# A hybrid encoder step on one core: values product with two heads in the column halves, and three smaller moves

## Chip, cores and metric

The kernel runs on one core of one Trainium2 chip. The metric is device time in microseconds (us), the median of the runs shown; lower is better.

## What is computed

One inference step of a one-layer streaming encoder on 2048 prompt frames and on 8 sampled streams of 16 frames, all float32, model width 1024. Three residual sub-layers follow one another: a mixer, a cross-attention into 256 memory tokens, and a squared-ReLU MLP. The change is in the mixer alone. Cut to it:

```python
q, k, v, u = in_proj(rms_norm(xp, g_mix_pre), w_in)      # 8 heads of 64; u = a * sigmoid(b), 512 channels
s = einsum('bnqhd,bnkhd->bnhqk', qc, kb) * Dh ** -0.5    # each 64-frame chunk against a 576-frame key band
s = where(key_valid, s + rel_bias(table, q_off, k_off), NEG_INF)
o = einsum('bnhqk,bnkhd->bnqhd', softmax(s), vb)
c = depthwise_conv(pad(u, 30), w_dw) + b_dw              # width 31, causal
c = silu(group_layer_norm(c, ln_g, ln_b))
xp = xp + rms_norm(concat([rms_norm(o), rms_norm(c)]) @ w_out, g_mix_post)
```

A sampled stream attends to 128 cached frames and its own 16, and its convolution continues from 30 cached rows.

## The kernel before, in words

**Layout of the work.** The 16 prompt tiles of 128 frames and the one tile of sampled frames form four query blocks, QT: tiles 0 to 3 and the sampled tile, then 4 to 7, 8 to 11 and 12 to 15. For each block the input projection (`glu`, `qk`, `vv`) multiplies the transposed rows by column pieces of w_in. Each product is made in three passes of high and low halves (`mm3`, line 122; `split`, lines 94 and 95, makes the halves: ACT the high, DVE or POOL the low). Queries, keys and values go to the DRAM scratch tensors Qd, Kd and Vd.

**Order.** A planner (`Plan`) holds closures with due times; `add(t0, t1, fns)` spreads a list of them evenly over an interval, `run` calls them in order of time, and the constants PAR give the intervals. So the input projection of block q + 1, the attention of block q, and the convolution taps are interleaved on PE, DVE, ACT and POOL, each of which takes its work in order. Loads and most stores are issued on SP's queue, also in order. A framework places the tiles into a fixed number of buffers per tag and adds the waits; a tile whose buffers are all in use waits for one to come free, and so does what stands behind it on the same queue.

**Attention (`attn`, lines 533 to 623).** For block q and head h, `attn_load` (line 533) loads the queries (tag aq), the keys in two transfers (ak), the values (av) and the bias table (ab); every one of these tags has two buffers. The planner's list goes through the 8 heads, each with its 4 query tiles, one step per tile. `scores` (551) makes up to 640 scores for 128 queries in the one score tile in PSUM (tag sc, one buffer of two banks); DVE adds the bias and takes the minimum (570), ACT exponentiates (573). One step later `xpose` (579) transposes the probabilities 128 x 128 at a time into one of three transpose banks (tag tp), and ACT copies them out into a tile of tag apt (two buffers). Two steps later `values` (592) multiplies with the probabilities as weights and the head's values as the moving operand:

```python
    for j in range(nj):
        nc.tensor.matmul(oc[:, i, :], pt[:, j, :], vt[:, jo + j, :], start=j == 0, stop=j == nj - 1)
```

Here pt[:, j, :] is 128 x 128 and vt[:, jo + j, :] is 128 x 64; a float32 matmul appears in the profile as two records. After a head's fourth tile DVE takes reciprocals of the sums (604) and scales the result (606), and after every second head SP stores 128 columns into the scratch catd (609). `attn` adds the load of head h + 1 behind step 2 of head h.

**Convolution.** `glu` (316) writes u of block q behind 30 carried columns in a tile of 542. For q above 0, POOL copies them from the carry tile ucar (326), and at the end of the block POOL copies the last 30 columns into ucar (340). The 31 taps of each of four channel groups run on DVE (452), block by block. Eight u tiles exist.

**Sampled streams (`sattn`, lines 629 to 719).** Before block 0's attention, eight streams are taken in turn. `sattn_load` (654) loads a stream's cached keys (tag att, shared with the biased scores) and values (tag sv), POOL places the queries into a zero-padded tile (664), PE transposes the keys (667) and ACT copies them out (668). The products with four heads side by side (677 and 703) use column tiles 32 wide, set by `tile_position`.

**After the mixer's attention** come the output projection (`out_norm`, `out_t`, `out_b`), which begins during block 3's attention, the memory attention and the MLP.

## Time and profile before

| what | value |
|---|---|
| median of 3 runs | 3248.61 us (3243.86 to 3252.39) |
| profiled execution, its own time | 3248.02 us |
| its span, first to last instruction | 3246.2 us |
| PE (matmul) busy | 3116.6 us, 96% |
| PEld (weight load) busy | 2659.1 us, 82% |
| DVE busy | 1820.0 us, 56% |
| ACT busy | 1234.3 us, 38% |
| POOL busy | 604.6 us, 19% |
| mean granted TensorE clock | 0.984 of full |

PE is TensorE's matmul, PEld its weight load, which overlaps PE; DVE is VectorE, ACT ScalarE, POOL GpSimd, SP SyncE, and a trailing q (SPq) means the engine's instruction queue. Matmuls are pipelined and their ends are modelled, so a PE that is shown busy need not be PE at its peak. The shares are means over stages that differ; a table by stage says more. L599 is line 599 of the kernel before.

### The profile page before, as it was taken

The numbers are of one execution on the slowest core, as the hardware profiler recorded it, in microseconds if no ns is written. First come the engines' busy times: TensorE is split into PE (matmuls) and PEld (weight loads), VectorE is DVE, ScalarE is ACT, GpSimd is POOL, SyncE is SP. The second block draws the span as 40 slices with busy tenths as digits, with TensorE's granted clock in tenths as the row PEclk, the third lists the DMA queues.
The fourth block names the chain that finished last, engine by engine and source line by source line (L and its number), as shares of the span: only waits on it lengthen the run. The fifth ranks groups of instructions, "written<-read, shape, count | busy, mean of one in ns | idle before, by whom it ended". The sixth has DMA issues, their size and how long they took to land. (4 is left out here: it accounts for less than half of the span.)

```text
span 3246.2 us, 44496 instructions
## 1 busy us (share of the span) xinstructions
PE 3116.6 (96%) x16628; PEld 2659.1 (82%) x16628; DVE 1820.0 (56%) x2807; ACT 1234.3 (38%) x2498; POOL 604.6 (19%) x655
## 2 busy tenths in 40 slices
PE   7987989999899999999999999999999999999998
PEld 7875878979798768788888999988888888888887
DVE  6797989788534435433335444456445544465444
ACT  3233454544554435322234232334334333343332
POOL 4346253442222320122211000002000200020000
PEclk9998999999899999999999999999999999999999
DMA  5464666747865565222224222234233433243222
GB/s 190 127 181 136 185 180 166 194 126 188 248 166 170 187 210 174 88 72 65 62 91 140 82 75 82 75 110 153 88 104 120 143 104 101 88 141 122 91 95 75
DMA packets 295062, 421.49 MB, mean 130 GB/s; under 512 B 54968, under 2 KB 163520, under 8 KB 294774
## 3 DMA queue, kind: packets, MB, share of 16 engines
q1 hardware_dynamic: 286286, 387.71, 40.4%
q0 software_dynamic: 8560, 30.94, 2.4%
q8 instruction: 131, 2.15, 0.3%
q14 instruction: 85, 0.70, 0.1%
HBM read 352.93 MB, written 69.52 MB: 130 GB/s over the span
## 5 line engine op out<-in xcount | busy, mean ns | idle before, releaser
L122 PE MATMUL pu<-xT,wu 128*128 128x512 f32 (+1 forms) x3840 | 756.6, 358 | 0.3 <-ACT wu L94 0.3
L122 PE MATMUL pd<-wd,h 128*128 128x512 f32 x3264 | 750.1, 390 | 0.1
L122 PEld LDWEIGHTS pu<-xT,wu 128*128 128x128 f32 x3840 | 660.2, 188 | 92.8 <-ACT wu L94 0.8
L122 PEld LDWEIGHTS pd<-wd,h 128*128 128x128 f32 x3264 | 611.4, 188 | 127.9 <-DVE y L1348 0.5
L122 PE MATMUL pm<-xT,w 128*128 128x512 f32 (+3 forms) x1992 | 427.1, 366 | 12.7 <-POOL w L95 4.2
L452 DVE SCALAR_TENSOR_TENSOR acc<-u,wdT,acc 128x512 f32<-128x512 f32 x480 | 429.4, 895 | 6.2
L103 POOL TENSOR_SCALAR nm<-nss 128x1 f32<-128x1 f32 x103 | 30.8, 299 | 2009.6 <-ACT nsq L132 1069.8
L122 PEld LDWEIGHTS pm<-xT,w 128*128 128x128 f32 x1992 | 341.5, 196 | 58.7 <-POOL w L95 5.2
L94 ACT ACTIVATE wd<-wst 128x512 fp32r<-128x512 f32 x256 | 159.9, 632 | 429.7 <-PE pd L122 365.3
L95 POOL TENSOR_TENSOR w<-wst,w 128x512 fp32r<-128x512 f32 x154 | 235.6, 1546 | 350.6 <-ACT w L94 320.5
L1348 DVE TENSOR_TENSOR y<-pd,y 128x512 f32<-128x512 f32 x238 | 163.8, 688 | 207.1 <-PE pd L122 207.1
L1330 DVE SCALAR_TENSOR_TENSOR hh<-pu,r 128x512 f32<-128x512 f32 (+1 forms) x160 | 96.9, 609 | 325.1 <-ACT r L1329 324.9
L1329 ACT ACTIVATE r<-pu 128x512 f32<-128x512 f32 (+1 forms) x160 | 84.0, 529 | 370.5 <-PE pu L122 364.8
L95 DVE TENSOR_TENSOR wu<-wst,wu 128x512 fp32r<-128x512 f32 x256 | 170.8, 690 | 83.9 <-ACT wu L94 82.6
L122 PE MATMUL pm<-wo,cT 128*128 128x512 f32 x816 | 200.2, 397 | 0.0
L95 DVE TENSOR_TENSOR wd<-wst,wd 128x512 fp32r<-128x512 f32 x256 | 178.9, 723 | 32.9 <-ACT wd L94 32.1
L94 ACT ACTIVATE wu<-wst 128x512 fp32r<-128x512 f32 x256 | 157.5, 631 | 96.3 <-DMA wst<-w_ffn_up 62.6
L122 PE MATMUL y<-mo,pT 128*128 128x512 f32 x768 | 186.8, 397 | 0.0
L122 PE MATMUL sc<-m,xT 128*128 128x512 f32 x768 | 182.0, 392 | 0.3 <-ACT xT L94 0.2
L122 PEld LDWEIGHTS pm<-wo,cT 128*128 128x128 f32 x816 | 151.1, 188 | 33.6 <-issue 2.9
L122 PEld LDWEIGHTS y<-mo,pT 128*128 128x128 f32 x768 | 142.8, 188 | 33.1
L122 PEld LDWEIGHTS sc<-m,xT 128*128 128x128 f32 x768 | 142.9, 188 | 30.7 <-DVE xT L95 0.5
(248 smaller groups left out, 3597.1 us busy)
## 6 DMA issues: line engine op xcount, KB each, us to landing
wst<-w_ffn_up SPq DMA_DIRECT2D x256, 256.0 KB, 3.2
wst<-w_ffn_down SPq DMA_DIRECT2D x256, 256.0 KB, 3.0
wst<-w_in SPq DMA_DIRECT2D x160, 256.0 KB, 3.3
ak<-Kd SPq DMA_DIRECT2D x48, 512.0 KB, 6.7
ab<-biasd SPq DMA_DIRECT2D x32, 320.0 KB, 4.2
cx<-catd SPq DMA_DIRECT2D x17, 512.0 KB, 5.3
x1d<-oy POOLq DMA_DIRECT2D x17, 512.0 KB, 6.4
nx<-x1d SPq DMA_DIRECT2D x17, 512.0 KB, 3.6
```

What stands on the lines that cost most here:

```text
L94: nc.scalar.activation(hi, src, AF.Copy)
L95: return (lo_eng or nc.vector).tensor_sub(lo, src, fr(hi))
L103: nc.gpsimd.tensor_scalar(m, ss, 1.0 / count, EPS, op0=ALU.mult, op1=ALU.add)
L122: self.nc.tensor.matmul(out, lhs(a), rhs(b), start=first and n == 0, stop=last and n == 2)
L452: i = nc.vector.scalar_tensor_tensor(o, s, wdT[:, c, w:w + 1], o, op0=ALU.mult, op1=ALU.add)
L1329: nc.scalar.activation(r, pm, AF.Relu)
L1330: nc.vector.scalar_tensor_tensor(hh, pm, 0.0, r, op0=ALU.max, op1=ALU.mult)
L1348: nc.vector.tensor_add(y, pm, y)
```

## The change

Five parts go together.

1. The values product swaps its operands: the head's values are the weights (64 columns) and the transposed probabilities move (128 columns). Two heads of a pair g are multiplied alternately, one into the lower 64 partitions of oc and one into the upper 64, with `tile_position=(0, x * HD)`. The result is transposed, heads' dimensions by queries, and fills a whole PSUM bank. After the fourth query tile ACT copies it out, and a new closure `heads_out` transposes it back tile by tile on PE into a transpose bank, from which DVE scales it for both heads at once; SP stores it.
2. The steps of the two heads of a pair are interleaved in the order ORDER. `values` of a query tile follows two steps behind the second head's scores, `heads_out` three steps behind the last. Heads 0 and 1 of a block are loaded first; head h + 2 is loaded behind the last score step of head h. Tags av and apt have four buffers in place of two.
3. The carry tile ucar goes. The first 30 columns of a block's u are copied, at the start of the block, from the tile of the block before.
4. A sampled stream's cached keys are loaded one stream ahead (`sattn_keys`, from tag av), its values go to tag ab, and the query tile to tag aq.
5. ACT, not POOL, places the sampled queries.

```diff
--- before.py
+++ after.py
...
@@ -258,7 +258,6 @@
-            ucar = [vp.tile([P, 30], F32, tag=f"ucar{c}", name=f"ucar{c}", bufs=1) for c in range(4)]
@@ -323,7 +322,7 @@
                             else:
-                                nc.gpsimd.tensor_copy(U[q, c][:, 0:30], ucar[c])
+                                nc.gpsimd.tensor_copy(U[q, c][:, 0:30], U[q - 1, c][:, 512:542])
                         nc.scalar.activation(U[q, c][:, 30 + c0:30 + c0 + npr], pm[:, :npr], AF.Copy, scale=0.5)
@@ -336,8 +335,6 @@
-                        if c0 + n >= 512 and q < 3:
-                            nc.gpsimd.tensor_copy(ucar[c], u[:, 512:542])
@@ -540,12 +537,13 @@
                         nc.sync.dma_start(fr(kt)[j * HD:(j + 1) * HD, :, :nk * P], Kd[h, :, :, k0 * P:(k0 + nk) * P].rearrange("a d t -> d a t"))
-                    vt = mp.tile([P, 8, HD], F32, tag="av", name="av")
+                    vt = mp.tile([P, 8, HD], F32, tag="av", name="av", bufs=4)
                     nc.sync.dma_start(vt[:, :nk, :], Vd[k0 * P:(k0 + nk) * P, h].rearrange("(j p) d -> p j d", p=P))
                     nc.sync.dma_start(bt, biasd[h])
-                    ss = mp.tile([P, 4], F32, tag="ass", name="ass")
-                    KQ[q, h] = (qt, kt, vt, bt, ss, k0)
+                    if h % 2 == 0:
+                        SUM[q, h // 2] = mp.tile([P, 4, 2], F32, tag="ass", name="ass")
+                    KQ[q, h] = (qt, kt, vt, bt, SUM[q, h // 2], k0)
                 return fn
@@ -570,7 +568,7 @@
-                    nc.scalar.activation(pr[:, :n], tt[:, :n], AF.Exp, bias=mn, scale=-1.0, accum_out=ss[:, i:i + 1])
+                    nc.scalar.activation(pr[:, :n], tt[:, :n], AF.Exp, bias=mn, scale=-1.0, accum_out=ss[:, i, h % 2:h % 2 + 1])
@@ -579,7 +577,7 @@
                 nj = n // P
-                pt = mp.tile([P, 5, P], F32, tag="apt", name="apt")
+                pt = mp.tile([P, 5, P], F32, tag="apt", name="apt", bufs=4)
                 for a, b in ((0, min(nj, 3)), (3, nj)):
@@ -587,39 +585,64 @@
                             nc.tensor.transpose(tp[:, (j - a) * P:(j - a + 1) * P], pr[:, j * P:(j + 1) * P], self.ident)
                         dst, src = pt[:, a:b, :], tp.rearrange("p (j q) -> p j q", j=b - a)
                         nc.scalar.activation(dst, src, AF.Copy)
-                READY.append((q, h, i, pt, nj, jo))
-            def values():
-                q, h, i, pt, nj, jo = READY.pop(0)
-                qt, kt, vt, bt, ss, k0 = KQ[q, h]
-                if i == 0:
-                    OC[q, h] = ps.tile([P, 4, HD], F32, tag="oc", name="oc")
-                oc = OC[q, h]
-                for j in range(nj):
-                    nc.tensor.matmul(oc[:, i, :], pt[:, j, :], vt[:, jo + j, :], start=j == 0, stop=j == nj - 1)
-                if i == 3:
-                    if h % 2 == 0:
-                        A[q] = mp.tile([P, 4, P], F32, tag="a", name="a")
-                    r = mp.tile([P, 4], F32, tag="ar", name="ar")
+                READY[q, h, i] = pt, nj, jo
+            def values(q, g, i):
+                def fn():
+                    if i == 0:
+                        OC[q, g] = ps.tile([P, 4, P], F32, tag="oc", name="oc")
+                    oc = OC[q, g]
+                    hs = [READY.pop((q, 2 * g + x, i)) + (KQ[q, 2 * g + x][2],) for x in range(2)]
+                    nj = hs[0][1]
+                    for j in range(nj):
+                        for x, (pt, _, jo, vt) in enumerate(hs):
+                            nc.tensor.matmul(oc[x * HD:(x + 1) * HD, i, :], vt[:, jo + j, :], pt[:, j, :], start=j == 0, stop=j == nj - 1,
+                                             tile_position=(0, x * HD))
+                    if i == 3:
+                        ot = mp.tile([P, 4, P], F32, tag="t512", name="ot")
+                        nc.scalar.activation(ot, oc, AF.Copy)
+                        OC[q, g] = ot
+                return fn
+            def heads_out(q, g):
+                def fn():
+                    ot, ss = OC.pop((q, g)), SUM.pop((q, g))
+                    tp = ps.tile([P, 512], F32, tag="tp", name="tpv", bufs=TPB)
+                    for i in range(4):
+                        nc.tensor.transpose(tp[:, i * P:(i + 1) * P], ot[:, i, :], self.ident)
+                    r = mp.tile([P, 4, 2], F32, tag="ar", name="ar")
                     nc.vector.reciprocal(r, ss)
-                    c = (h % 2) * HD
-                    nc.vector.tensor_tensor(A[q][:, :, c:c + HD], oc, r.unsqueeze(2).to_broadcast([P, 4, HD]), op=ALU.mult)
-                    if h % 2:
-                        t0 = QT[q][0]
-                        nc.sync.dma_start(catd[t0 * P:(t0 + 4) * P, (h - 1) * HD:(h + 1) * HD].rearrange("(i p) c -> p i c", p=P), A[q])
+                    A = mp.tile([P, 4, P], F32, tag="a", name="a")
+                    nc.vector.tensor_tensor(A.rearrange("p i (x d) -> p (i x) d", x=2), tp.rearrange("p (n d) -> p n d", d=HD),
+                                            r.rearrange("p i x -> p (i x)").unsqueeze(2).to_broadcast([P, 8, HD]), op=ALU.mult)
+                    t0 = QT[q][0]
+                    nc.sync.dma_start(catd[t0 * P:(t0 + 4) * P, g * P:(g + 1) * P].rearrange("(i p) c -> p i c", p=P), A)
+                return fn
+            ORDER = ((0, 0), (0, 1), (1, 0), (0, 2), (1, 1), (0, 3), (1, 2), (1, 3))

             def attn(q):
-                fns = [attn_load(q, 0)]
-                for n in range(4 * H + 2):
-                    h, i = n // 4, n % 4
-                    if n < 4 * H:
-                        fns.append(scores(q, h, i))
-                    if 0 < n <= 4 * H:
+                steps = [(2 * g + x, i) for g in range(H // 2) for x, i in ORDER]
+                fns = [attn_load(q, 0), attn_load(q, 1)]
+                for n in range(len(steps) + 3):
+                    if n < len(steps):
+                        fns.append(scores(q, *steps[n]))
+                    if 0 < n <= len(steps):
                         fns.append(xpose)
-                    if n > 1:
-                        fns.append(values)
-                    if i == 2 and h + 1 < H:
-                        fns.append(attn_load(q, h + 1))
+                    if 1 < n < len(steps) + 2:
+                        h, i = steps[n - 2]
+                        if h % 2:
+                            fns.append(values(q, h // 2, i))
+                    if n > 2:
+                        h, i = steps[n - 3]
+                        if h % 2 and i == 3:
+                            fns.append(heads_out(q, h // 2))
+                    if n < len(steps):
+                        h, i = steps[n]
+                        if i == 3 and h + 2 < H:
+                            fns.append(attn_load(q, h + 2))
                 return fns


@@ -641,7 +664,7 @@
-                SA["q"] = q = mp.tile([P, 4, P], F32, tag="saT", name="saq", bufs=1)
+                SA["q"] = q = mp.tile([P, 4, P], F32, tag="aq", name="saq")
@@ -650,18 +673,24 @@
                 z = mp.tile([P, 2, 4, 32], F32, tag="sqb", name="sz", bufs=1)
                 nc.gpsimd.memset(z, 0.0)
                 SA["z"] = [z[:, n] for n in range(2)]
+                sattn_keys(0)
+            def sattn_keys(b):
+                SA["ck", b] = ck = mp.tile([P, DA], F32, tag="av", name="sck", bufs=4)
+                nc.sync.dma_start(ck, I["cache_attn_k"][0, b].rearrange("t h d -> t (h d)"))

             def sattn_load(b):
                 def fn():
-                    ck = mp.tile([P, DA], F32, tag="att", name="sck")
-                    nc.sync.dma_start(ck, I["cache_attn_k"][0, b].rearrange("t h d -> t (h d)"))
-                    cv = mp.tile([P, DA], F32, tag="sv", name="scv")
+                    ck = SA.pop(("ck", b))
+                    if b + 1 < 8:
+                        sattn_keys(b + 1)
+                    cv = mp.tile([P, 640], F32, tag="ab", name="scv")[:, :DA]
                     nc.sync.dma_start(cv, I["cache_attn_v"][0, b].rearrange("t h d -> t (h d)"))
                     K, Z = SA["k"][b % 2], SA["z"][b % 2]

                     for j in range(2):
                         rs = slice(j * HD, (j + 1) * HD)
-                        nc.gpsimd.tensor_copy(Z[rs, :, j * 16:(j + 1) * 16], SA["q"][rs, :, b * 16:(b + 1) * 16])
+                        nc.scalar.activation(Z[rs, :, j * 16:(j + 1) * 16], SA["q"][rs, :, b * 16:(b + 1) * 16], AF.Copy)
                     pt = ps.tile([P, 512], F32, tag="tp", name="pt", bufs=TPB)
                     for p in range(4):
                         nc.tensor.transpose(pt[:, p * P:(p + 1) * P], ck[:, p * P:(p + 1) * P], self.ident)
@@ -695,7 +724,7 @@
-                    PT = mp.tile([P, 2, P], F32, tag="apt", name="spt")
+                    PT = mp.tile([P, 2, P], F32, tag="apt", name="spt", bufs=4)
...
```

Two hunks that give the setup tiles of tag av four buffers as well, and one that renames dictionaries, are left out.

## Rows read from the trace of the kernel before

**Rows 1.** Stages: us from the start, length; busy (records) per engine; clock; DMA share; GB/s.

```profile
205.00:315.00 110.00, 86.45 (x546) 65.00 (x545) 91.31 (x151) 42.83 (x91) 64.76 (x68) 0.94 0.56 161
315.00:430.00 115.00, 107.00 (x726) 94.77 (x725) 108.44 (x196) 56.66 (x152) 34.54 (x24) 0.99 0.69 185
430.00:680.00 250.00, 232.26 (x1448) 206.32 (x1447) 204.51 (x285) 116.91 (x253) 114.12 (x92) 0.97 0.63 167
680.00:850.00 170.00, 159.24 (x1083) 145.77 (x1083) 138.29 (x218) 82.23 (x184) 44.74 (x36) 0.97 0.68 183
850.00:1000.00 150.00, 143.20 (x905) 129.54 (x906) 65.60 (x123) 85.15 (x202) 33.85 (x46) 0.94 0.65 177
```

The engines of these rows are, in this order, PE, PEld, DVE, ACT and POOL.

**Rows 2.** The same stages, instructions of line 599 alone: PE, PEld, clock, DMA.

```profile
315.00:430.00 115.00, 21.28 (x152) 20.24 (x152) 0.99 0.69 185
430.00:680.00 250.00, 41.60 (x328) 40.74 (x328) 0.97 0.63 167
680.00:850.00 170.00, 39.36 (x320) 39.19 (x320) 0.97 0.68 183
850.00:1000.00 150.00, 42.20 (x320) 41.42 (x320) 0.94 0.65 177
```

**Rows 3.** Timeline of PE, merged: start us, length us, line, tiles, count.

```profile
564.85 1.23 PE L599 MATMUL oc<-av,apt 128*128 128x64 f32 x10
565.89 0.83 PE L566 MATMUL sc<-ak,aq 128*128 128x320 f32 x4
566.56 0.71 PE L587 MATMUL tpa<-ident,apr 128*128 128x128 f32 x5
...
845.78 0.49 PE L587 MATMUL tpa<-ident,apr 128*128 128x128 f32 x3
846.11 2.34 PE L599 MATMUL oc<-av,apt 128*128 128x64 f32 x20
```

**Rows 4.** Waits of DVE, 430 to 680: us in total, times, longest us.

```profile
DVE lnd L506 <- POOL lnr L105: 9.7, 7, 2.1
```

**Rows 5.** Timeline of PE around a sampled stream's values product.

```profile
259.11 0.43 PE L703 MATMUL ov<-scv,spt 128*32 128x128 f32 x8
259.35 0.40 PE L703 MATMUL ov<-svn,spt 128*32 128x128 f32 x8
259.69 0.49 PE L486 MATMUL pt<-cent,acc 128*128 128x128 f32 x2
```

**Rows 6.** Line 703: duration in ns, min/median/max, first and last start.

```profile
L703 PE MATMUL ov<-svn,spt x64: 272/273/423, 238.3 to 316.5; 128*32 128x128 f32 x64
```

**Rows 7.** Timeline of DVE in block 3's attention, two score steps three apart.

```profile
922.08 0.82 DVE L570 CUSTOM_DVE_ANT_0 att<-sc,ab 128x640 f32<-128x640 f32 x1 [0.22 <-PE sc L566]
...
929.58 0.82 DVE L570 CUSTOM_DVE_ANT_0 att<-sc,ab 128x640 f32<-128x640 f32 x1 [0.32 <-ACT apr L573]
```

**Rows 8.** Groups by line, 0 to 1300: busy us, mean ns; idle before, releaser.

```profile
L606 DVE TENSOR_TENSOR a<-oc,ar 128x256 f32<-128x256 f32 x32 | 13.4, 419 | 15.1 <-PE oc L599 15.0
L570 DVE CUSTOM_DVE_ANT_0 att<-sc,ab 128x512 f32<-128x512 f32 x8 | 5.5, 682 | 0.0
L488 ACT ACTIVATE lnd<-pt 128x512 f32<-128x512 f32 x17 | 10.0, 592 | 25.4 <-PE pt L486 13.4 <-DMA catd<-lnd 6.8 <-PE pt L667 5.2
L340 POOL COPY ucar<-u 128x30 f32<-128x30 f32 x12 | 5.4, 454 | 25.5 <-DVE u L335 25.5
```

**Rows 9.** Waits of SP's queue, 850 to 1000.

```profile
SPq L544 <- PE oc L599: 45.6, 4, 14.9
```

**Rows 10.** Timeline of SP's queue: one head's load.

```profile
878.64 0.36 SPq L539 DMA_DIRECT2D aq<-Qd  x1
879.04 1.25 SPq L542 DMA_DIRECT2D ak<-Kd  x2
```

**Rows 11.** DMA issues by line: count, KB each, median us to landing.

```profile
ak<-Kd SPq DMA_DIRECT2D x48, 512.0 KB, 6.7
```

**Rows 12.** Waits of PE, 205 to 315.

```profile
PE pt L667 <- DMA sck<-cache_attn_k: 10.1, 5, 3.1
```

More of the change, by code (lines that the diff above doesn't have):

```diff
@@ L231, in bias_tables @@
                 for h in range(H):
-                    hk = mp.tile([P, 2, P], F32, tag="av", name="hk")
+                    hk = mp.tile([P, 2, P], F32, tag="av", name="hk", bufs=4)
                     for m in range(2):
@@ L243, in bias_tables @@
                     nc.sync.dma_start(biasd[h], bt)
-                hs = mp.tile([P, 2, P], F32, tag="av", name="hs")
+                hs = mp.tile([P, 2, P], F32, tag="av", name="hs", bufs=4)
                 nc.sync.dma_start(hs[:, 0, :].rearrange("p (h q) -> p h q", h=H), view(extd, P, [[1, P], [768, H], [1, 16]]))
@@ L528, in lns @@
                 return fns
-            A, KQ, PEND, READY = {}, {}, [], []
+            KQ, SUM, PEND, READY = {}, {}, [], {}
             def attn_load(q, h):
```

## Prediction, made before the change was run

> **What bounds the kernel now.** I first cut the span into the stages in which the changed code runs [rows 1]: the sampled streams' attention (205 to 315 us), the band attention of query blocks 0, 1 and 2, each interleaved with the input projection of a later block (315 to 430, 430 to 680, 680 to 850), and that of block 3, interleaved with the output projection (850 to 1000). The reader is to see which engine is nearly full. From 315 to 850 both PE and DVE are: DVE is busy 108.4 of 115, 204.5 of 250 and 138.3 of 170 us, because the convolution taps run there. From 850 to 1000 there are no taps; DVE is busy 65.6 of 150 us, PE 143.2. Everything after 1000 us is outside the change; I take it to move as a block.
>
> Next I asked how much of these stages is the values product of line 599 [rows 2]: 152, 328, 320 and 320 matmul records, 1120 in all. The merged timeline [rows 3] gives their pace: ten take 1.23 us, twenty 2.34, so one per 0.111 us and 124.3 us of PE for all. Three transposes take 0.49 us, five 0.71: 0.11 each.
>
> The waits say what DVE does in its idle time. In 430 to 680 its largest wait is for POOL, 9.7 of 45.5 idle us [rows 4], a round trip that a faster PE does not shorten. So PE time saved in the last stage should show, before it only partly.
>
> **Values as weights.** Removed are the 1120 records with 128 weight columns and 64 moving ones. Added are as many with 64 weight columns and 128 moving, two heads side by side in the column halves: 560 rounds of two. The trace has no tile 64 columns wide, but four tiles 32 wide with 128 moving columns [rows 5]: 16 records in four rounds, the first at 259.11, the last ending at 259.75 and lasting 0.27 [rows 6], so starting at 259.48. Three rounds in 0.37 us make 0.12 a round, loading of weights included. The bounds are 0.111 (the pace of one matmul) and 0.222 (two in turn); I take 0.12, the row nearest in shape. 560 x 0.12 = 67.2, which saves 57.1 us.
>
> The Trainium skill, TensorE: Matmul & The Clock Gate, Part 3, lists as seen that weights are loaded beside matmuls in flight only where the row group differs, which column halves do not. By that a round would be a load and then its matmuls, the 0.222 of the rival on halves in turn, and the sum 3260; by the row it is 0.12, and the sum is the one below. Four rounds with all their loads at 0.12 do not agree with the rule.
>
> Entering and leaving the column tiles costs something too. The next whole-array matmul starts at 259.69 [rows 5], 0.21 after the last round began, where a round takes 0.12: 0.09 lost. I take as much on the way in, rounded to 0.2 for both. Four blocks, four pairs of heads and four query tiles make 64 visits: 12.8 us, or twice that if other work is put between the parts of a visit. The result now comes out transposed, so each of the 16 pairs needs four transposes back: 64 x 0.11 = 7.0 us. Net on PE: 57.1 - 12.8 - 7.0 = 37.3 us less, 0.0333 per record, with ends of 54 less (rounds of 0.111, free switches) and 20 more (rounds of 0.222).
>
> How much reaches the end depends on the stage. By [rows 2] the shares are 5.1, 10.9, 10.7 and 10.7 us.
> In 850 to 1000 PE is the bound, but there is one score buffer: scores take 0.83 us [rows 3], the reduction that frees their buffer 0.82 [rows 7], so steps that follow closely cannot come faster than 1.65 us and two hand-overs, against 2.26 us of PE work today (values 1.04, scores 0.67, transposes 0.55, by the starts and paces of [rows 3]). Two thirds: 7.1. In 680 to 850 and 430 to 680 DVE idles 19% and 18%, partly for reasons that stay; half: 5.4 and 5.5. In 315 to 430 DVE idles only 6.6 us; a fifth: 1.0. Sum: 19.0 us.
>
> **Scaling moves to the pair.** DVE had 32 scalings of 0.419 us [rows 8], 13.4 us. Now there are 16 of 512 columns out of PSUM, which I price by the 128x512 reduction of 0.682: 10.9. 2.5 us less, half of it in stages where DVE is full: 1.3. Sixteen reciprocals of a few elements go too; left out. ACT gains 16 copies of 0.592 us [rows 8], 9.5 us, which its idle time hides (busy 341 of 685 us from 315 to 1000, rows 1). What they hold is scarcer: a 512-column buffer shared with the gates and the normalisation, and one of three transpose banks until DVE has scaled. Between 0 and 3 us; I take 1.
>
> **Short lags and buffers.** A visit comes two steps after the second head's scores, as it did after a head's own. Four values buffers remove SP's wait for a values slot, 45.6 us in the last stage [rows 9]; behind it stood the bias table, output rows and the next head's load. PE did not wait for those, so I count nothing; if SP is then blocked elsewhere, the rival on loads has the price.
>
> **Head loads come closer to their use.** Queries and keys have two buffers. A head's load could start when the head before last was scored, five steps ahead of use; with two heads interleaved the buffer is freed three steps ahead. A load takes: queries issued at 878.64, the second keys transfer at about 879.67 [rows 10], which lands 6.7 us later [rows 11], at 886.4, so 7.7 us, and with the scores that free the buffer 8.5. At the 18 places in blocks 1 to 3 where a load will now stand, three steps took 7.5 us at the narrowest [rows 7]; one other is under 10 us. If these and the start of block 0 run late by one or two us each, that is 4 us. Bounds are 0 and the rival's price. Behind a waiting load SP holds the projection's weights; they are asked for three columns of work ahead, which covers it.
>
> **Cached keys a stream ahead.** PE waited 10.1 us for these transfers [rows 12]. The stage has DVE busy 91.3 of 110 us too, so I take half: 5.0, between 0 and 10. The small query copies go from POOL to ACT, busy 42.8 of 110 there: nothing, as long as ACT is not late for the next scores.
>
> **The carry.** Twelve copies of 0.454 us leave POOL, with 25.5 us of waiting in front of them [rows 8]; the other copy reads the old block itself. POOL is busy 34.5 of 115 and 44.7 of 170 where it matters, so I count nothing; up to 5 us are possible where weight halves stood behind the wait.
>
> **The sum** is made against the profiled execution, 3248.0 us, 0.6 below the median of the three runs: 3248.0 - 19.0 - 1.3 + 1 + 4 - 5.0 = 3227.7, taken as 3228.
>
> **The rivals.**
> Full landing: 37.3, DVE's 2.5 and the 10 us of cached keys all arrive and no load is late: 3248.0 - 49.8 = 3198. For it speaks that PE is busy above 92% in every stage from 315 us; against it DVE's 451 busy us of 535 before 850, with taps that stay.
> DVE takes over: nothing lands between 315 and 850, only 7.1 and 5 elsewhere, against 5 of new cost: 3248.0 - 7.1 = 3241. For it speaks 108.4 of 115; against it, that DVE idles 45.5 and 31.7 us in the two longer stages.
> The loads decide, and the kernel is slower: half of the 24 loads inside the runs are late by 4 us, 48 us of idle PE, since PE takes its work in order and a waiting score holds the projection up too: 3248.0 - 24 + 48 = 3272. It decides where three steps come under 8.5 us, or where SP reaches the load later than the buffer is free by more than the window has to spare. For it speaks the lead cut from five steps to three; against it that most windows were 11 to 25 us.
> Halves in turn, so that the change does not do what it says: a round takes 0.222, values stay at 124.3 and switches and transposes add 19.8 to PE, two thirds of which land: 3248.0 + 13.2 - 1.3 - 5 + 5 = 3260. The next weights would not load while the other half's matmul runs. Rows 5 speak against it; that they show quarters, not halves, leaves it open.
>
> **How the numbers follow.** About 0.3%, 9.7 us, is what a measurement of this kernel tells from no change: 3238.9 to 3258.4. The forecast has 0.50 (its own range 3206 to 3243: faster 0.47, same 0.03), full landing 0.15 (faster), DVE takes over 0.17 (faster 0.05, same 0.11, slower 0.01), the loads 0.11 (slower), halves in turn 0.07 (same 0.03, slower 0.04). Together faster 0.67, same 0.17, slower 0.16. The range is 3194 to 3263: down to full landing, up past halves in turn; it leaves out most of the loads' case.
>
> **What would show it.** Right: pairs of values matmuls that start within some 0.01 us of each other, one round per 0.12; the stage of block 3 shorter by some 7 us; no wait of the sampled key transposes for transfers; DVE above 85% busy between 315 and 850. Wrong: scores of a new head waiting for the keys transfer (the loads), values records at 0.111 each in turn (halves), blocks 0 to 2 as long as before with DVE fuller (DVE takes over), or time moving after 1000 us, where I expect nothing.

## The result: slower by 0.8%, and the profile after

The changed kernel took 3275.21 us, median of 4 runs (3272.08 to 3279.3); the kernel before, on the same chip, 3249.95. The ratio is 1.0082, interval 1.007 to 1.0094. I had forecast 3228 with a range to 3263.

| what | after | before |
|---|---|---|
| profiled execution, its own time | 3273.22 us | 3248.02 us |
| its span | 3271.4 us | 3246.2 us |
| PE busy | 3103.2 us, 95% | 3116.6 us, 96% |
| PEld busy | 2601.8 us, 80% | 2659.1 us, 82% |
| DVE busy | 1823.4 us, 56% | 1820.0 us, 56% |
| ACT busy | 1246.2 us, 38% | 1234.3 us, 38% |
| POOL busy | 589.4 us, 18% | 604.6 us, 19% |
| granted TensorE clock | 0.981 | 0.984 |

PE has 13 us less to do, where I had counted 37, and the kernel is 25 us longer. The table by stage, as in [rows 1] (PE, PEld, DVE, ACT, POOL, clock, DMA, GB/s):

```profile
205.00:315.00 110.00, 86.40 (x533) 63.43 (x532) 92.48 (x162) 44.84 (x104) 63.22 (x47) 0.90 0.54 161
315.00:430.00 115.00, 105.34 (x707) 86.66 (x708) 108.59 (x181) 56.57 (x149) 31.92 (x22) 0.98 0.70 190
430.00:680.00 250.00, 223.24 (x1465) 188.26 (x1461) 200.60 (x272) 117.33 (x255) 108.76 (x86) 0.98 0.61 162
680.00:850.00 170.00, 155.02 (x1086) 131.25 (x1086) 139.59 (x209) 81.23 (x185) 45.76 (x37) 0.96 0.65 170
850.00:1000.00 150.00, 125.62 (x813) 100.56 (x810) 61.54 (x109) 81.25 (x187) 28.26 (x38) 0.90 0.67 187
```

In 430 to 680 PE is busy 9 us less than before and DVE 4: PE is idle instead. In 850 to 1000 it is busy 125.6 of 150 us where it was 143.2, at a clock of 0.90 where it was 0.94. The values product alone, as in [rows 2]:

```profile
315.00:430.00 115.00, 16.20 (x156) 9.83 (x158) 0.98 0.70 190
430.00:680.00 250.00, 22.84 (x329) 17.76 (x324) 0.98 0.61 162
680.00:850.00 170.00, 21.90 (x304) 17.00 (x306) 0.96 0.65 170
850.00:1000.00 150.00, 25.18 (x280) 17.38 (x276) 0.90 0.67 187
```

86.1 us in place of 144.4, so the product is cheaper, as meant. These sums flatter it: the last record of every visit is modelled past the start of what follows, and the trace has 138 visits (values records with no other matmul between them) before and 98 after. Counted from start to start, the product takes 120.3 us before and 84.3 after. Where PE waits now shows in its timeline (start, length, line, tiles, count; in brackets the idle time before and what ended it):

```profile
295.81 0.66 PE L564 MATMUL sc<-ak,aq 128*128 128x128 f32 x2 [7.19 <-issue]
...
547.87 2.10 PE L122 MATMUL pm<-xT,w 128*128 128x512 f32 x8
554.09 1.43 PE L564 MATMUL sc<-ak,aq 128*128 128x320 f32 x4 [4.12 <-DVE amn L568]
...
570.54 1.31 PE L600 MATMUL oc<-apt,av 128*64 128x128 f32 x20
...
849.75 1.31 PE L600 MATMUL oc<-apt,av 128*64 128x128 f32 x20
858.61 1.11 PE L613 MATMUL tpv<-ident,ot 128*128 128x128 f32 x4 [7.54 <-ACT ot L604]
```

L564 is the scores, L568 the reduction, L571 the exponential, L600 the values, L604 the copy, L613 the transposes back. Twenty records of the values product take 1.31 us, 2.34 before [rows 3]. Three waits stand out: 7.2 us for block 0's first score, 4.1 us for a reduction, 7.5 us for the copy. What DVE did ahead of the reduction:

```profile
546.11 5.92 DVE L449 SCALAR_TENSOR_TENSOR acc<-u,wdT,acc 128x512 f32<-128x512 f32 x4
551.95 0.68 DVE L95 TENSOR_TENSOR e<-pm,e 128x512 fp32r<-128x512 f32 x1
552.55 0.74 DVE L449 SCALAR_TENSOR_TENSOR acc<-u,wdT,acc 128x512 f32<-128x512 f32 x1
553.21 0.81 DVE L568 CUSTOM_DVE_ANT_0 att<-sc,ab 128x640 f32<-128x640 f32 x1
```

The scores were there at 547.6; the reduction came 5.6 us later, behind four taps (one of 0.74 us, three of 1.66 to 1.75), a split and one more tap. And ACT ahead of the copy:

```profile
854.90 1.06 ACT L94 ACTIVATE wo<-wos 128x1024 fp32r<-128x1024 f32 x1 [6.55 <-DMA wos<-w_out]
857.01 1.06 ACT L94 ACTIVATE wo<-wos 128x1024 fp32r<-128x1024 f32 x1 [1.05 <-DMA wos<-w_out]
857.98 0.58 ACT L604 ACTIVATE ot<-oc 128x512 f32<-128x512 f32 x1
```

The copy was ready at about 851 and stood behind two pieces of the output weights that had not landed. From 846 to 856 PE was busy 5.1 of 10 us; from 856 to 866 the granted clock was then 0.50, the lower of its two levels (1.2 of 2.4 GHz). In the kernel before, with PE busy 7.3 of the same 10 us, it was 0.83.

### The profile page after: what moved, and what is told of

Same layout as the page of the kernel before. It is cut to its first block, busy times and chain, and to the rows that moved or that the text cites. A ratio compares the mean times of both kernels' runs of the same rounds, so it can differ in the third digit from the quotient of the medians.

```text
span 3271.4 us, 44510 instructions
## 1 busy us (share of the span) xinstructions
PE 3103.2 (95%) x16692; PEld 2601.8 (80%) x16692; DVE 1823.4 (56%) x2775; ACT 1246.2 (38%) x2530; POOL 589.4 (18%) x627
```

## Experiments

Kernels of one group ran on one chip beside the kernel before, whose median was 3246.7, 3247.0, 3248.7, 3247.7 and 3247.9 us in the five groups. Diffs are against the changed kernel unless another is named. Where the time goes is told by five points of each trace (starts), as differences to the kernel before, in us: the last result of the sampled streams (320.1 before), the last matmul of the input projection (830.3), the first of the output projection (879.6), of the memory attention's queries (1014.6) and of the MLP (1726.4). These are single executions, and the whole times of one kernel spread over some 10 us, so a difference of a few us decides nothing by itself.

| kernel | streams | projection's end | output proj. | queries | MLP |
|---|---|---|---|---|---|
| small parts only | -2.5 | +0.9 | -0.5 | +0.1 | -1.5 |
| operands, heads in turn | -6.4 | +1.0 | +2.3 | +0.8 | +2.3 |
| order alone, even steps | -3.3 | +5.4 | +10.7 | +12.4 | +11.2 |
| changed kernel | -6.3 | +7.0 | +14.3 | +21.4 | +23.7 |
| cached keys only | -11.2 | -4.2 | -7.4 | -8.5 | -8.5 |

### First group: which part costs

**Small parts only** puts the attention's functions of the kernel before back; the carry, the sampled streams and four av and apt buffers stay.

```diff
-                steps = [(2 * g + x, i) for g in range(H // 2) for x, i in ORDER]
...
+                for n in range(4 * H + 2):
+                    h, i = n // 4, n % 4
...
```

> The values part is undone (old operands, heads one after the other, scaling straight from PSUM); carry, sampled streams and the four values buffers stay. Theory (the loss lies in the values part: a copy on ACT that PE waits for, and DVE taking what PE saves): the sampled stage ends 5 to 7 us early as in the changed kernel and keeps some of it, so 3240 to 3250, and no stall of 7 us at 850. Rival (the small parts moved other work out of place and cost the time): 3265 to 3280.

Measured: 3245.0 us, ratio 0.9995 (0.9984 to 1.0005). The whole loss comes with the values part and its order.

**The order alone**: interleaved steps and loads, with the probabilities as weights again.

```diff
-                            nc.tensor.matmul(oc[x * HD:(x + 1) * HD, i, :], vt[:, jo + j, :], pt[:, j, :], start=j == 0, stop=j == nj - 1,
-                                             tile_position=(0, x * HD))
+                            nc.tensor.matmul(oc[:, x, i, :], pt[:, j, :], vt[:, jo + j, :], start=j == 0, stop=j == nj - 1)
...
-                            fns.append(heads_out(q, h // 2))
```

> Two heads interleaved in the new order with the new load places, buffers and carry, but the probabilities are the weights again and DVE scales straight from PSUM: no copy on ACT, no transposes back. PE does 125 us of values again. Theory (copy on ACT in PE's way): 3245 to 3262, slower by what PE does more, without the 7.5 us stall before block 3. Rival (interleaved order and loads three steps ahead are the loss): 3275 or more, since order and loads are the same and PE has more to do.

Measured: 3256.96 us, 1.0029 (1.0019 to 1.0038). The order costs some 10 us by itself.

**The copy on DVE**, and **the output weights asked for earlier**:

```diff
-                        nc.scalar.activation(ot, oc, AF.Copy)
+                        nc.vector.tensor_copy(ot, oc)
```

> The changed kernel, with the pair's result copied out of PSUM by DVE in place of ACT: 16 copies of some 0.7 us move to DVE. Theory: the copy no longer stands behind the output weights' halves, which wait for transfers; the 7.5 us stall at 850 goes and with it the low clock behind it, 3258 to 3268. Rival (order and loads): 3275 to 3285, 11 us more on DVE where it is full and nothing gained.

```diff
-    o=-13.2, os=16.3, wa=14.8, wb=24.7, ta0=21.5, tb0=165, ln0=36.1,
+    o=-13.2, os=16.3, wa=5.0, wb=24.7, ta0=21.5, tb0=165, ln0=36.1,
```

> The changed kernel, with the eight output weight pieces due from 5.0 to 24.7 in place of 14.8 to 24.7, twice as far apart, so that ACT waits less for each transfer. Theory: the stall of PE for the copy before block 3 shrinks from 7.5 to under 3 us, 3262 to 3270. Rival: 3272 to 3279, as the changed kernel.

Measured: 3274.74 (1.0085, 1.0069 to 1.01) and 3271.44 us (1.0073, 1.0057 to 1.0089). Neither theory holds. With the copy on DVE the 7.5 us wait is gone and nothing is won: the projection already ends 10 us later than in the changed kernel. The earlier weights leave a wait of 6.7.

### Second group: taps, way back, lumps

**Half the taps**, once in each kernel:

```diff
-                    return [first] + [tap(w) for w in range(1, 31)]
+                    return [first] + [tap(w) for w in range(1, 31, 2)]
```

> The kernel before with every second convolution tap left out (16 of 31 taps per channel group are computed). It is the base for the run beside it: DVE has some 230 us less to do between 315 and 850 us. If DVE held up PE there, this kernel is faster than the kernel before by some 15 to 30 us; if PE is the bound, by less than 8.

> The changed kernel with every second convolution tap left out (16 of 31 taps per channel group are computed). To be read against the kernel before with the same taps left out. Theory (taps on DVE take what PE saves): with DVE half empty PE's saving lands, the score steps no longer wait behind taps, and this kernel is level with or up to 15 us faster than its base, and at the end of the input projection 10 to 25 us ahead of it. Rival (the order and the copy with its transposes cost PE time of their own, whatever DVE does): it is 20 to 30 us slower than its base, as with all taps.

Measured: 3214.44 us (0.9893, 0.9878 to 0.9908) and 3215.53 (0.9894, 0.9875 to 0.9912), so level. The first is faster than either case had it. I took the two as the theory's proof, too early: the last group shows what they are made of.

**Without the way back**:

```diff
-                        ot = mp.tile([P, 4, P], F32, tag="t512", name="ot")
-                        nc.scalar.activation(ot, oc, AF.Copy)
...
-                        nc.tensor.transpose(tp[:, i * P:(i + 1) * P], ot[:, i, :], self.ident)
```

> The changed kernel without the way back: DVE scales straight out of the values buffer, the copy by ACT and the four transposes of each pair are left out (so the attention's result reaches the output projection untransposed). Theory (the copy, the transposes and the wait for the copy behind the output weights are what the new operands cost on top of the order): 3250 to 3258 us, no wait of PE for the copy at 850 us. Rival (the switches into and out of the column halves and the fuller DVE cost it): 3266 us or more. If PE's saving lands once the way back is gone: 3240 or less.

Measured: 3269.52 us, 1.0066 (1.005 to 1.0083), some 5 us below the changed kernel's 1.0082. The time is the rival's: the way back is a small part. That switches and a fuller DVE are the rest is not shown by it.

**Even steps** (against the order alone):

```diff
-                        if h % 2:
-                            fns.append(values(q, h // 2, i))
+                        fns.append(values(q, *steps[n - 2]))
```

> The interleaved order and the two loads ahead with the old operands, as in the earlier run of the order alone (3257 us), but each head's values two steps behind its own scores, so that every step has ten values matmuls in place of twenty in every second one. Theory (the lumps cost the 10 us: a step without values leaves PE waiting for the reduction): 3245 to 3250 us. Rival (two heads' loads at the start of a block and three steps' lead cost them): 3255 to 3259 us.

Measured: 3260.38 us, 1.0038 (1.0025 to 1.0051). The lumps are not it. PE's waits from 836 to 900 in this kernel (total us, times, longest):

```profile
PE tpa L585 <- ACT apr L571: 6.9, 2, 4.0
PE sc L564 <- DMA ak<-Kd: 6.8, 1, 6.8
```

One score of block 3 waits 6.8 us for keys: with the heads interleaved both key buffers are held to the end of block 2. SP asked for the block's first keys at 839 us, where before it did so at 821.

### Third group: the late keys

**Heads in turn with the new operands** (a step's transposes also go behind its values product):

```diff
-            ORDER = ((0, 0), (0, 1), (1, 0), (0, 2), (1, 1), (0, 3), (1, 2), (1, 3))
+            ORDER = tuple((x, i) for x in range(2) for i in range(4))
...
-                pt = mp.tile([P, 5, P], F32, tag="apt", name="apt", bufs=4)
+                pt = mp.tile([P, 5, P], F32, tag="apt", name="apt", bufs=5)
...
-                        if i == 3 and h + 2 < H:
-                            fns.append(attn_load(q, h + 2))
+                        if i == 2 and h + 1 < H:
+                            fns.append(attn_load(q, h + 1))
```

> The changed kernel with its new operands, but the two heads of a pair scored one after the other as before, head h + 1 loaded behind the third step of head h as before, and five buffers for the transposed probabilities so that the pair can still be multiplied together. Theory (with the heads interleaved both key buffers are held to the end of a block, so the next block's first keys come some 14 us later and collide with the output weights): the keys of block 3 are asked for before 830 us again, the output weights land in 5 to 7 us in place of 9.7, and the time is 3250 to 3262 us. If the new operands then gain as well: below 3246. Rival (the operands, with copy, transposes and switches, cost it, in any order): 3268 us or more.

Measured: 3254.78 us, 1.0016 (1.0007 to 1.0025): some 20 of the 27 us are back. The keys went out at 820 us and the output weights landed in 6.5 us.

**The kernel before with a late first load** (against the kernel before):

```diff
+                    if q == 3 and h == 0:
+                        dk = mp.tile([P, 2, 1024], F32R, tag="ak", name="dk")
+                        nc.sync.dma_start(fr(dk)[:HD, :, :64], Kd[h, :, :, :64].rearrange("a d t -> d a t"))
```

> The kernel before, with one small dummy keys tile allocated ahead of block 3's first head, so that this head's keys take the buffer of block 2's last head and can be loaded only when that head is scored; no work but a 32 KB transfer is added. Theory (the late first load of block 3 is what the interleaved order costs at 830 to 900 us): 5 to 11 us slower than the kernel before, the output weights land later than 5.5 us and the output projection starts 5 to 11 us later. Rival (it is something else in the order): within 3 us.

Measured: 3252.71 us, 1.0008 (1.0 to 1.0017). The output weights did land later, 8.4 us against 5.5, yet the output projection's start moved only 1 us against the projection's end. So late weights alone do not cost it. The keys were asked for at 831 us here, not at 839, and no score waited for them, so this tests the late keys only in part.

**A third buffer of keys and queries** (against even steps), and **the split two pieces behind its load**:

```diff
-                    kt = mp.tile([P, 2, 1024], F32R, tag="ak", name="ak")
+                    kt = mp.tile([P, 2, 1024], F32R, tag="ak", name="ak", bufs=3)
-                    qt = mp.tile([P, 512], F32R, tag="aq", name="aq")
+                    qt = mp.tile([P, 512], F32R, tag="aq", name="aq", bufs=3)
...
```

> The order alone with the old operands and each head's values behind its own scores (3260 us with two buffers of keys and queries), now with three buffers of keys and of queries, and two and three in place of four of the probabilities and values to make the room. Theory (late loads for want of a free buffer cost the order's 10 to 13 us): 3245 to 3251 us. Rival (the order costs it by how the steps fall): 3256 us or more.

```diff
-                    self.split(w[:, 0], w[:, 1], s)
-                    OP["w"].append(w)
+                    WO.append((w, s))
+                    if k > 1:
+                        wo_split(k - 2)
...
```

> The changed kernel with the split of each output-weights piece put two pieces behind its load, so that ACT and DVE do not stand with attention work behind a piece that has not landed. Theory (those two queues pass the lateness on to PE): the 7.5 us wait for the copy is gone, 5 to 10 us are won, 3263 to 3268 us. Rival (the late keys themselves hold the attention): within 3 us of the changed kernel's 3273 to 3275.

Measured: 3258.43 us (1.003, 1.0018 to 1.0041) and 3270.24 (1.0068, 1.0054 to 1.0081). With three buffers the wait for keys is gone and the stretch from the projection's end to the output projection is 2 us longer than before, not 5; but block 0's attention ends 12 us later (444.0 against 431.7), with fewer buffers for probabilities and values. With the lag the copy still comes 7.8 us late.

### Fourth group: taps again

> The new operands with the heads in turn (3254.8 us with all taps), with every second convolution tap left out, as in the two earlier runs; its base is the kernel before with the same taps left out, 3214.4 us. Theory (what PE saves in 315 to 850 us turns into waits behind taps on DVE): with DVE half empty it lands, 3190 to 3204 us, 10 to 24 us below the base. Rival (the copy, the transposes and the switches eat it on PE and ACT): 3210 to 3222 us, as far above the base as with all taps.

> The interleaved order alone, old operands and even steps (3260.4 us with all taps), with every second tap left out; base 3214.4 us. Theory (the order costs its 10 to 13 us in the last block, where no taps run): 3222 to 3228 us. Rival (it costs it by the reductions' place among the taps): 3210 to 3219 us.

Both have the tap diff above. Measured: 3195.12 us (0.9841, 0.9827 to 0.9854) and 3207.84 (0.988, 0.9866 to 0.9893), the first within its theory's bounds, the second below both of its cases. Their base, the kernel before with half the taps, did not hold the small parts, and that decides; the last group mends it.

**Block 3 in turn** (against even steps):

```diff
-                steps = [(2 * g + x, i) for g in range(H // 2) for x, i in ORDER]
+                steps = [(2 * g + x, i) for g in range(H // 2) for x, i in ORDER[q]]
...
```

> The interleaved order alone, old operands and even steps (3260.4 us), but block 3's heads in turn again, with their loads as before. Theory (the order's cost arises in block 3, where PE has little but attention until the output weights are there): 3247 to 3253 us, level with the kernel before. Rival (it arises in blocks 0 to 2 or at the start of block 3, whose first keys still wait for block 2's last two heads): 3256 us or more.

Measured: 3257.44 us, 1.0033 (1.0021 to 1.0046): the rival's time. A score of block 3 still waits 7.1 us for keys, since block 2's last two heads hold both buffers.

**In turn, without the way back** has the diff of the way back above, against heads in turn.

> The new operands with the heads in turn (3254.8 us), without the way back: the copy by ACT and the four transposes of each pair are left out, and DVE scales straight out of the values buffer, so the attention's result reaches the output projection untransposed. Theory (the way back is what the new operands cost in this order): 3244 to 3250 us. Rival (the cost is the wait behind DVE, which scales as before): 3252 to 3257 us.

Measured: 3252.58 us, 1.0013 (1.0004 to 1.0022), level with heads in turn (1.0016). The way back costs nothing there that can be measured.

### Fifth group: the square, and the cached keys

> The change without its values part (carry, sampled streams, four values and probabilities buffers; 3245.0 us with all taps), with every second convolution tap left out. It completes a square: with half the taps the kernel before took 3214.4 us and the new operands with the heads in turn 3195.1. Their traces differ by 14 us already at the end of the sampled streams. Theory (with DVE half empty PE's saving in the values product lands): 3206 to 3214 us, so that the operands are worth 11 to 19 us there. Rival (the sampled streams' part is what lands, and the operands' saving becomes waits for the reduction even with half the taps): 3195 to 3203 us, so that the operands are worth nothing to 8.

Measured: 3192.7 us, 0.9831 (0.9816 to 0.9847). That is below both cases and nearer to the rival: the operands are worth nothing. The square reads, in us and, since each group had its own chip, as ratios to the kernel before beside it:

| kernel | all taps | half the taps |
|---|---|---|
| before | 3247 to 3249 (1) | 3214.4 (0.9893) |
| small parts | 3245.0 (0.9995) | 3192.7 (0.9831) |
| and new operands, in turn | 3254.8 (1.0016) | 3195.1 (0.9841) |
| and order, old operands, even | 3260.4 (1.0038) | 3207.8 (0.9880) |
| and both | 3275.2 (1.0082) | 3215.5 (0.9894) |

By the ratios, against the small parts, the operands with the heads in turn cost 7 us with all taps and 3 with half, each uncertain by about 5; the order 14 and 16; both 28 and 20. So half the taps do not let the operands' saving reach the end, and the order's price does not come from taps. What becomes of the saving shows in the stretch of blocks 0 to 2, cut in each trace at the same work: from the last result of the streams to the last matmul of the input projection. With half the taps (PE busy first), small parts:

```profile
289.70:778.30 488.60, 475.19 (x3127) 429.35 (x3127) 298.57 (x500) 242.28 (x561) 171.53 (x137) 0.99 0.69 183
```

and with the new operands, heads in turn:

```profile
287.10:771.10 484.00, 461.96 (x3150) 390.80 (x3150) 293.62 (x477) 247.14 (x574) 170.48 (x135) 0.99 0.70 186
```

PE is busy 13.2 us less, the stretch is 4.6 us shorter, and PE is idle 8.6 us more, at a DVE that works only 61% of the time. PE's waits in these stretches, small parts:

```profile
PE sc L563 <- DVE amn L567: 5.8, 8, 1.5
```

and new operands:

```profile
PE sc L564 <- DVE amn L568: 15.0, 14, 2.6
```

9.2 us more of waiting for the reduction that frees the one score buffer: two thirds of the saving. The third that did land was gone again by the first matmul of the MLP, which comes 56.0 us earlier than in the kernel before with the small parts and 56.3 with the new operands. With all taps nothing lands. Small parts:

```profile
317.80:831.50 513.70, 484.54 (x3129) 434.75 (x3128) 439.28 (x672) 242.77 (x559) 182.38 (x137) 0.97 0.65 174
...
PE sc L563 <- DVE amn L567: 17.0, 8, 7.1
```

new operands, heads in turn:

```profile
314.00:831.70 517.70, 473.47 (x3152) 396.81 (x3152) 437.79 (x648) 248.47 (x573) 177.63 (x135) 0.97 0.65 173
...
PE sc L564 <- DVE amn L568: 33.7, 19, 7.1
```

PE is busy 11 us less, waits 17 us more for the reduction, and the stretch is 4 us longer. These lengths are of single executions; the waits are the firmer part.

Part of this may come from multiplying the pair together, and not from the cheaper product. With the heads in turn a pair's values follow the second head, so 51 of 94 score steps of this stretch have no values product since the step before; with the small parts 16 of 93. Of the 34 us of waiting 24 stand before such steps, of the 17 us 13; with half the taps 9.6 of 15.0 and 0.8 of 5.8. No run separated the two with the new operands.

**Cached keys only** (against the kernel before): the streams' values and queries keep their own buffers; tag av has four.

```diff
-                    ck = mp.tile([P, DA], F32, tag="att", name="sck")
-                    nc.sync.dma_start(ck, I["cache_attn_k"][0, b].rearrange("t h d -> t (h d)"))
+                    ck = SA.pop(("ck", b))
+                    if b + 1 < 8:
+                        sattn_keys(b + 1)
```

> The kernel before with a single part of the change: a sampled stream's cached keys come one stream ahead, in tag av with four buffers; the streams' values and queries stay in the buffers of their own that the change took away. Theory (the 5 to 6 us won in the sampled streams are lost again because block 0's first head now waits for buffers shared with the streams, the 7.2 us wait at its first score): 3241 to 3245 us. Rival (they are lost to DVE's taps whatever the buffers): 3246 to 3251 us.

Measured: 3239.16 us, ratio 0.9974 (0.9965 to 0.9983), 8.7 us faster than before and faster than every other kernel with all taps. The largest waits of PE from 205 to 330 us in the small-parts kernel:

```profile
PE sc L563 <- issue: 7.2, 1, 7.2
PE ov L706 <- ACT spt L702: 5.4, 2, 4.6
```

and with the cached keys only:

```profile
PE ov L709 <- ACT spt L705: 7.0, 3, 5.2
PE sps L683 <- ACT sk L674: 6.0, 1, 6.0
```

The time is below the theory's range. The 7.2 us wait of block 0's first score is not there. What that score waited for stands in the small-parts kernel's timeline:

```profile
286.62 0.64 PE L680 MATMUL sps<-sk,sz 128*32 128x256 f32 x8
299.36 0.08 DVE L683 DVE_READ_ACCUMULATOR2_ANT smn<- 128x1 f32 x1
299.53 0.66 PE L563 MATMUL sc<-ak,aq 128*128 128x128 f32 x2 [7.18 <-issue]
```

The streams' scores (L680) and the band's (L563) use the same score tile, tag sc. DVE reduced the last stream's scores (L683) 12 us after they were there, behind taps, steps of the normalisation and another stream's result, and block 0's first score started 0.1 us after that. In the other kernels with all taps and the streams' part this score stands in PE's queue ahead of the products of the last two streams and holds them up; here it follows them. With the third buffer of queries alone among these it found the tile free, and the next score waited 7.4 us for DVE. With half the taps the wait is missing, and there the small parts are worth 20 us (0.9893 to 0.9831). So the wait is one for DVE's place in the queue. Why the order in PE's queue differs was not tried part by part: the carry, the streams' other buffers and the placing by ACT are all left out here.

## Why the prediction was wrong

**The matmul was right, the way in and out too cheap.** Pairs run side by side, 20 records in 1.31 us, so one round in 0.115 ((1.31 - 0.27) / 9), against 0.12 taken. Halves in turn fell. The Trainium skill, TensorE: Matmul & The Clock Gate, Part 3, has a line that lists weight loads beside matmuls in flight only for another row group; it does not agree with these rows: ten rounds of other column halves took 1.31 us with all twenty of their loads. The same Part of the Trainium skill also lets a load run ahead into a background weight buffer, and no run here tells whether that was the way. The switches I put at 64 visits of 0.2 us. Other work split them into 98 visits, the case that I named and did not take. In the trace the start of a values record follows a transpose of the probabilities by 0.20 us, where transposes follow each other by 0.11, and what comes after a visit starts 0.20 us after its last record, where rounds follow each other by 0.11 (medians). Counted from start to start, the product takes 84.3 us where I had 80.0 with the switches, the records just before a visit take some 10 us more, and the transposes back 6.4 where I had 7.0. So PE saved about 19 us, not 37.3. (The upper end that I gave as 54 is 55 by its own terms; nothing hangs on it.)

**The step that failed is "How much reaches the end".** I let a fifth to two thirds of PE's saving land, by the idle share of DVE. With all taps none of it did, at a DVE that is 85% busy: in blocks 0 to 2 PE is busy 11 us less and the stretch is 4 us longer. With half the taps, at 61%, a third landed there and was lost behind it. DVE's share of busy time did not tell this. The single score buffer does: a score waits for the last reduction, and less PE work between two scores means that PE arrives earlier. I had worked out this chain, 1.65 us and two hand-overs, for the last stage alone, and even there only as a discount. The 19.0 us of the sum were 0, and about -7 with all taps. Why they are negative stays open: the way back is not it (level without it, heads in turn), and the pair's steps without values are a rival that no run settled.

**Against the sum**, by the ratios: the small parts gave 2 us where I had 5.0; the operands, heads in turn, cost 7 where I had a gain of 19.3 (19.0 and 1.3, less 1); the order with its loads cost 21 more where I had 4. Together that is the 27 us of 1.0082, within rounding.

**The order had no term.** I priced the visits' lag and the loads, not the order as such; it costs 10 to 15 us with the old operands, and with the new ones 20. One part is seen: the first keys of block 3, late because both buffers are held, cost one wait of 5.6 to 7.5 us in each of the four kernels that have this order with old operands and two buffers. My "one or two us" for a block's start was this term, too small. The rest, most of it, stays open: every edit also moves instructions in the queues, and twice a wait that was removed in one place came back as a loss in another (the copy on DVE, the third key buffer).

**The rival of the loads** had the sign and, by luck, nearly the time, 3272: what happened is not 12 loads late by 4 us, but one late block start, with scores of a new head waiting 1.5 us in all in the changed kernel. "DVE takes over" had the nearest mechanism and gave 3241, as it had no cost for the order.

**ACT's copies**, put at 1 us because "its idle time hides" them, stood behind weights that had not landed, with ACT idle, and PE waited 7.5 us for one of them at 850. Taking the wait away gave nothing (copy on DVE) or 5 us (without the way back). An idle engine hides work only if nothing ahead in its queue waits.

**The cached keys** did what I wrote: the wait of [rows 12] is gone and the streams end 6.3 us earlier. The 5.0 us were lost at the next step, a first score 7.2 us late behind DVE, the very reason for which I had counted only half. Alone, the part gives 8.7.

**The carry and four buffers** I put at nothing. No run has them alone. All small parts together (0.9995) are 7 us behind the cached keys alone (0.9974), so the carry, the streams' other buffers and the placing by ACT together are not free, or bring the first score's wait with them.

## What to carry to other kernels

Before counting saved time on a busy engine, look at what its next wait is: where one buffer ties two engines in a chain, a shorter step can become a longer wait, here even with the other engine idle 39% of the time. Cut the stretches that you compare at the same work: in a fixed window idle time grows by what busy time falls, whatever happened. A change that holds two buffers at once must be followed to the next boundary, where the next block needs them. And run the parts of a bundle singly: here one of five was worth 8.7 us, and the others hid it.

## What the runs showed of the hardware that was not expected

The same tap takes 0.75 us or up to two and a half times that. In the changed kernel's trace the 318 taps of 512 columns that no POOL instruction overlaps take 0.73 to 0.75 us each. Of the other 162, 72 take over 1.3 us, up to 1.87, and POOL is busy for 59 to 100% of each of them. The slow taps ahead of the late reduction are among these:

```profile
546.88 1.66 DVE L449 SCALAR_TENSOR_TENSOR acc<-u,wdT,acc 128x512 f32<-128x512 f32 x1
546.24 1.75 POOL L95 TENSOR_TENSOR w<-wst,w 128x512 fp32r<-128x512 f32 x1 [1.20 <-ACT w L94]
...
550.28 1.75 DVE L449 SCALAR_TENSOR_TENSOR acc<-u,wdT,acc 128x512 f32<-128x512 f32 x1
550.22 1.26 POOL L95 TENSOR_TENSOR w<-wst,w 128x512 fp32r<-128x512 f32 x1 [0.52 <-ACT w L94]
```

No run took POOL's work away to show it as the cause.

Leaving out half of the taps was worth 33 us in the kernel before (ratio 0.9893). By its trace 19 of them are there by the end of the sampled streams, in a stage where PE was busy only 86 of 110 us [rows 1], and 16 more by the end of the input projection, where PE's idle time falls from 29 to 14 us. So DVE's taps hold PE up in both stages.
